# A hybrid decoder layer on one core: chunk after chunk in the first two steps of each group's MLP, post-norm products on GpSimd, and a longer first pause of the decode work

## The chip, the core and the metric

One core of a Trainium2 chip runs the whole layer as one program. The metric is the time of the program on the device, in microseconds (us). Every engine of the core (PE, the matrix engine; DVE, the vector engine; ACT, the scalar engine; POOL, GpSimd; SP, which here only issues transfers) works through its own list of instructions in order, and waits on semaphores for the others.

## The reference

The layer takes 2048 prompt tokens and 32 sample tokens (8 sequences of 4 tokens, each with its own state), 1024 wide, all in fp32. Cut to what matters here, with `x` the tokens and `p` a small input embedding:

```python
xn  = rms_norm(x, norm_mix_pre)
mix = concat(mlstm(xn @ w_in ...), sliding_window_attention(xn @ w_in ...)) @ w_out
x   = x + rms_norm(mix, norm_mix_post)          # a post-norm
u   = rms_norm(x, norm_ffn_pre)
f   = square(relu(u @ w_up)) @ w_down           # 1024 -> 4096 -> 1024
x   = x + rms_norm(f, norm_ffn_post)            # a post-norm
x   = x + sigmoid(x @ w_pgate) * (p @ w_pproj)
```

The sample tokens go through the same layer; their mLSTM and attention read and update given states and caches ("decode").

## The kernel before

**Stages.** The prompt is 16 blocks of 128 tokens. In a first phase, up to about 700 us, all blocks are projected with `w_in`, and mLSTM and attention are computed; their outputs go to DRAM. Then come three groups of two chunks: blocks 0-2 and 3-5 (group 0), 6-8 and 9-11 (group 1), 12-13 and 14-15 with the 32 sample rows (group 2). A group goes through `mix_mm` (the product with `w_out`, matmuls `mo`) and `mix_post` (post-norm, residual, pre-norm and transposes into the tile `ut`) of its first and then its second chunk, then `mlp`, then `gate_post` and `gate_mm` (matmuls `pt`, `pv`, `xt`, `pg`) of both chunks. In group 1 the decode work runs as a side job.

**Precision.** A fp32 number is kept as two fp32r parts, high (`h`) and low (`l`), and each product takes three matmuls (`mm3`, L145): high by high twice over the weights' two parts, and low by high. A helper makes the parts: ACT casts the high one (L228), DVE subtracts (L229); the weights have the same on ACT (L249) and in turns on POOL and DVE (L250).

**Weights.** A ring of 7 buffers holds 512 KB pairs [high|low] of weights. The first time that a weight is used, it is loaded raw on SP's queue, split, and its pair is stored to DRAM by POOL's queue (`wk<-w`, L275). Every later use loads the pair back on SP's queue (`w<-wk`, L282). A plan of all uses in order lets the loads run ahead as buffers come free.

**The MLP.** 16 steps `s` of 256 hidden columns each. For a chunk `ci`, `up(s, ci)` makes 48 matmuls into two tiles of 128 hidden columns; `hidden` takes each through relu and square on ACT (L1617, L1618) and the split (`hh` on ACT, `hl` on DVE); `down(s, ci, half)` makes the `dn` matmuls for one half of the output columns (`dn...t` for the second chunk of group 2, which is computed transposed and carries the sample rows). From step 2 on, `up_both` computes both chunks at once from seven products instead of eight. These need sums and differences of the two chunks' `ut`, which `sums` and `last_sum` make on DVE, ACT and, in groups 1 and 2, for one half of the columns on POOL (L1641 to L1675). The room for them is opened once the decode job is done.

**Steps 0 and 1** are plain. Before, they run in this order: up of step 0 for chunk 0 and its downs, up of step 0 for chunk 1 and its downs; then the sums are started; then up of step 1 for chunk 0, up of step 1 for chunk 1, `last_sum`, and the downs of both. In the sample group the hidden values of 16 of the sample rows are computed with chunk 0 and copied by POOL into chunk 1's tiles (L1624).

**Post-norm.** `finished(b, half, ...)` is called as soon as one half of block b's row is complete: ACT squares it with a running sum (L1441), and it is multiplied in place by the norm's weights (L1443), half 0 on POOL and half 1 on DVE. `rstd` adds on DVE (L1454) and takes the power -0.5 on POOL (L1455). `residual` scales the two halves and adds the block's input, on DVE (L1449).

**What sets the order.** PE's order is written out as the program is built: a model clock `pe.t` advances with each matmul, and side jobs (`swa`, `mls`, `tsp`, `dec`) are generators that yield a number of model microseconds; after each product `tick` runs the next piece of any side job whose time has come, and `drain` runs a job to its end. `tsp` holds post-norms and transposes, `dec` the decode job, which starts with one `yield DECW` and then runs `decode_mlstm` (its first matmuls are `dph`, transposes of the rows `hrow` that a POOL transfer at L1129 brings) and `decode_swa` (`daS`, `daT`, `daO`). The order on the other engines is decided by a scheduler when the program is built.

## Time and profile before

| what | value |
|---|---|
| median of 3 runs | 2674.26 us (2670.22 to 2679.49) |
| the profiled execution | 2676.5 us, of which the span is 2674.7 us |
| mean granted clock of TensorE | 0.981 |
| busy: PE / DVE / ACT / POOL | 95% / 55% / 36% / 25% of the span |
| first matmul of step 0 to first of step 2: group 0 / 1 / 2 | 75.37 / 92.93 / 73.23 us |

A row of the profile's timeline gives the start, the duration, the engine, the line, the operation with output and inputs, how many instructions are taken together, and in brackets how long the engine stood idle before it and what released it. PE is the engine that is nearly always busy, so its idle stretches, and the slow matmuls that follow some of them, are what can be won without computing less.

### The profile page before, as it was taken

The page shows a single profiled execution, that of the slowest core. Times are in us where ns is not written, and L with a number is a line of the kernel's source. Part 1 is how long each engine was busy: PE and PEld are TensorE (multiplying, and loading weights), DVE is VectorE, ACT ScalarE, POOL GpSimd, SP SyncE. Part 2 cuts the span into 40 slices and gives each one's busy share as a digit, 9 for nine tenths or more (in the row PEclk, how much of TensorE's full clock was granted, in tenths as well). Part 3 has the DMA queues.
Part 4 walks back from the last instruction along what each step waited for, and adds up shares of the span by engine and source line. Part 5 has one row for each costly group of instructions (what it writes and reads, how often), then busy time and mean ns, then how long its engine had stood idle before and what let it go on. Part 6 is the DMA issues. An engine that isn't in the chain of part 4 may idle for free.

```text
span 2674.7 us, 39114 instructions
## 1 busy us (share of the span) xinstructions
PE 2549.5 (95%) x14260; PEld 2212.9 (83%) x14260; DVE 1481.7 (55%) x3112; ACT 975.9 (36%) x2165; POOL 658.0 (25%) x936
## 2 busy tenths in 40 slices
PE   7899999998899999999998999999999998999998
PEld 6787878877688888888776789988888877999986
DVE  6675666664677655655735564444446345444443
ACT  5545344543455433444513432222223133222231
POOL 5311111111436666666513320000001012000010
PEclk9999999999999999999998999999999998999999
DMA  8765656666786666666987645555557885777786
GB/s 305 268 215 173 217 167 221 210 241 224 255 326 240 254 245 236 236 236 233 341 323 238 209 142 188 189 189 174 173 182 256 288 316 187 254 261 258 257 297 230
DMA packets 215186, 632.23 MB, mean 236 GB/s; under 512 B 24790, under 2 KB 58794, under 8 KB 214977
## 3 DMA queue, kind: packets, MB, share of 16 engines
q1 hardware_dynamic: 169552, 472.19, 52.0%
q0 software_dynamic: 45392, 157.50, 15.1%
q8 instruction: 113, 1.85, 0.3%
q14 instruction: 81, 0.66, 0.1%
q10 hardware_dynamic: 48, 0.03, 0.0%
HBM read 475.47 MB, written 155.25 MB: 236 GB/s over the span
## 4 chain that ended last, share of the span: by engine, by line
PE 74%; DVE 10%; DMA 6%; issue 4%; POOL 3%; ACT 2%; SPq 0%; POOLq 0%; DVEq 0%; ACTq 0%
PE dn L145 20%; PE up L145 20%; PE pg L145 5%; PE mo L145 5%; PE v L145 3%; DMA wk<-w 3%; PE qk L145 2%; DVE hl L229 2%; DMA w<-wk 2%; PE o L145 2%; PE gv L145 2%; PE qa L145 1%; PE aT L149 1%; PE aO L145 1%; PE pv L145 1%
## 5 line engine op out<-in xcount | busy, mean ns | idle before, releaser
L145 PE MATMUL dn<-w,hh 128*128 128x512 f32 x1792 | 566.6, 397 | 13.7 <-DVE f L1449 5.1
L145 PEld LDWEIGHTS dn<-w,hh 128*128 128x128 f32 x1792 | 333.2, 189 | 95.1 <-DVE f L1728 8.6
L1728 DVE TENSOR_TENSOR f<-f,dn 128x512 f32<-128x512 f32 x420 | 286.9, 687 | 222.0 <-PE dn L145 220.9
L145 PE MATMUL dn<-w,hl 128*128 128x512 f32 x896 | 355.5, 397 | 2.5 <-DVE hl L229 2.4
L1692 DVE TENSOR_TENSOR re<-up,re 128x384 f32<-128x384 f32 (+1 forms) x294 | 152.0, 517 | 326.4 <-PE up L145 326.4
L145 PEld LDWEIGHTS dn<-w,hl 128*128 128x128 f32 x896 | 169.0, 189 | 46.3 <-DVE hl L229 7.5
L1693 ACT COPY re<-up 128x384 f32<-128x384 f32 (+1 forms) x42 | 18.9, 450 | 414.8 <-PE up L145 414.8
L1617 ACT ACTIVATE re<-re 128x384 f32<-128x384 f32 (+1 forms) x168 | 83.2, 495 | 207.9 <-DVE re L1692 205.8
L229 DVE TENSOR_TENSOR hl<-re,hh 128x384 fp32r<-128x384 f32 (+1 forms) x192 | 137.7, 717 | 31.1 <-ACT hh L228 30.4
L275 POOL DMA_DIRECT2D wk<-w x242 | 134.0, 555 | 32.2 <-DVE w L250 29.2
L1443 POOL TENSOR_TENSOR f<-f,gffn 128x512 f32<-128x512 f32 x16 | 21.8, 1365 | 476.5 <-ACT j L1441 476.2
L250 POOL TENSOR_TENSOR w<-wr,w 128x512 fp32r<-128x512 f32 (+2 forms) x76 | 104.9, 1380 | 87.5 <-ACT w L249 86.6
L249 ACT CAST w<-wb 128x512 fp32r<-128x512 f32 x98 | 60.7, 621 | 173.2 <-PE dn L145 118.3
L249 ACT CAST w<-wr 128x512 fp32r<-128x512 f32 (+2 forms) x152 | 89.3, 598 | 85.6 <-PE up L145 34.3
L250 POOL TENSOR_TENSOR w<-wb,w 128x512 fp32r<-128x512 f32 x70 | 91.9, 1313 | 116.3 <-ACT w L249 115.8
L1618 ACT ACTIVATE re<-re 128x384 f32<-128x384 f32 (+1 forms) x192 | 95.1, 495 | 5.9
L228 ACT CAST hh<-re 128x384 fp32r<-128x384 f32 (+1 forms) x192 | 92.8, 483 | 6.8
L1043 ACT ACTIVATE s<-s,swt 128x257 f32<-128x257 f32 (+1 forms) x128 | 63.4, 497 | 77.5 <-DVE swt L1040 76.4
L1037 DVE CUSTOM_DVE_ANT_0 s<-aS,cst,sink 128x256 f32<-128x256 f32 (+1 forms) x128 | 57.0, 473 | 59.4 <-PE aS L145 59.2
L1624 POOL CAST hh<-hh 128x16 fp32r<-128x16 f32 x32 | 8.0, 249 | 319.0 <-ACT hh L228 319.0
L145 PE MATMUL up<-t0h,w 128*128 128x384 f32 (+1 forms) x336 | 85.1, 320 | 0.0
L145 PE MATMUL up<-t1h,w 128*128 128x384 f32 (+1 forms) x336 | 85.1, 320 | 0.0
(1537 smaller groups left out, 6530.7 us busy)
## 6 DMA issues: line engine op xcount, KB each, us to landing
w<-wk SPq DMA_DIRECT2D x692, 512.0 KB, 4.7
wk<-w POOLq DMA_DIRECT2D x238, 512.0 KB, 6.6
wr<-in_w_down_dram SPq DMA_DIRECT2D x64, 256.0 KB, 7.7
wb<-in_w_up_dram SPq DMA_DIRECT2D x28, 512.0 KB, 6.8
w<-wk SPq DMA_DIRECT2D x20, 528.0 KB, 4.4
x<-in_x_prompt_dram SPq DMA_DIRECT2D x16, 512.0 KB, 5.2
y<-yd SPq DMA_DIRECT2D x32, 256.0 KB, 7.1
xr<-in_x_prompt_dram SPq DMA_DIRECT2D x16, 512.0 KB, 6.3
```

What stands on the lines that cost most here:

```text
L145: ins = self.pe.matmul(out, lhsT, rhs, start=start, stop=stop)
L228: act.copy(hi, src)
L229: dve.tensor_tensor(lo, src, hi.bitcast(F32), ALU.subtract)
L249: act.copy(hi, src)
L250: (eng or weng()).tensor_tensor(lo, src, hi.bitcast(F32), ALU.subtract)
L275: here(put(self.kept[key], t.bitcast(U32)))
L1037: dve.tensor_tensor_reduce(s_[:, s, lo : 2 * P], pS[:, s, lo:], bias[:, j, lo:], 1.0 if s == 0 else 0.0625, sink[:, h : h + 1], ALU.add, A ...
L1043: act.activation(e_, e_, AF.Exp, bias=nm[:, s : s + 1], accum_out=sm[:, s : s + 1])
L1617: act.activation(t, src, AF.Relu)
L1618: act.square(t, t)
L1692: add = lambda out, a, b: dve.tensor_tensor(out, a, b, ALU.add)
L1728: dve.tensor_tensor(out(i), out(i), ps[i], ALU.add)
```

## The change

Three things are changed.

- **MLP order.** Steps 0 and 1 are done for chunk 0 first: up and downs of step 0, up and downs of step 1. Then the side jobs are drained, the room for the sums is opened and `sums` is started, and the same four passes are done for chunk 1. `last_sum` follows. The weights of the two steps are thus taken twice: 32 ring tiles a group in place of 20. The downs of step 1 now also begin with three blocks' matmuls on the first hidden tile (`ahead`), as those of step 0 did. In the sample group the 16 rows' hidden values are kept in small tiles between the chunks, with twice as many copies on POOL.
- **Post-norm products.** All products of L1443 go to POOL.
- **Decode's first pause**, `DECW`, is 12 model microseconds in place of 5.

```diff
-FAST = 2, 2, 2
+FAST = 2
-DECW = 5.0
+DECW = 12.0
...
-            for s in range(STEPS):
-                if s >= FAST[gi]:
+            for s in (*range(FAST), *range(STEPS)):
+                if s >= FAST:
...
-                for half in (0, 1, 0, 1) if s == 0 else (0, 1):
+                for half in (0, 1):
...
-        eng = (pool, dve)[half]
-        eng.tensor_tensor(v, v, g[:n, half * 512 : half * 512 + 512], ALU.mult)
+        pool.tensor_tensor(v, v, g[:n, half * 512 : half * 512 + 512], ALU.mult)
...
-            if sample and ci == 1:
-
-                for y, z in zip(hid[0, ft], hid[1, ft]):
-                    pool.tensor_copy(z[:, W : W + HS], y[:, W - HS : W].bitcast(F32))
+            if sample:
+
+                for e, y in enumerate(hid[ci, ft]):
+                    if ci == 0:
+                        t = hid["s", ft, e] = small.tile([P, HS], F32, tag="hs", name=f"hs{e}{nm}", bufs=8)
+                        pool.tensor_copy(t, y[:, W - HS : W].bitcast(F32))
+                    else:
+                        pool.tensor_copy(y[:, W : W + HS], hid["s", ft, e])
...
-            ahead = 3 if s == 0 else 1
+            ahead = 3 if s < FAST else 1
...
-        X = None
-        for s in range(STEPS):
-            hid = {}
-            fast = s >= FAST[gi]
-            if not fast:
-                wu = ring.take(4)
-            if s == 0:
-
-                up(s, 0, wu, hid)
-                for half in range(2):
-                    down(s, 0, half, down_weights(), hid)
-                pe.drain(tsp)
-                up(s, 1, wu, hid)
-                for half in range(2):
-                    down(s, 1, half, down_weights(), hid)
-                continue
-            if s == FAST[gi] - 1:
+        X, hids = None, []
+
+        for ci in range(2):
+            if ci == 1:
+                pe.drain(tsp)
                 pe.drain(dec)
                 es_lp.close()
                 es_t = ExitStack()
                 tp = es_t.enter_context(tc.tile_pool(name="tp", bufs=1, side="right", reuse_waits="tile"))
                 ring.wide = es_t.enter_context(tc.tile_pool(name="wide", bufs=WIDE, side="right", reuse_waits="tile"))
                 tsp.add(sums())
-            if fast:
-                up_both(s, X, hid)
-            else:
-                up(s, 0, wu, hid)
-                up(s, 1, wu, hid)
-                if s == FAST[gi] - 1:
-                    pe.drain(tsp)
-                    last_sum()
+            for s in range(FAST):
+                if ci == 0:
+                    hids.append({})
+                up(s, ci, ring.take(4), hids[s])
+                for half in range(2):
+                    down(s, ci, half, down_weights(), hids[s])
+        pe.drain(tsp)
+        last_sum()
+        for s in range(FAST, STEPS):
+            hid = {}
+            up_both(s, X, hid)
```

Line numbers behind the edits shift: L1443 of before is L1442 after, L1449 is L1448, and from `hidden` on they are three higher.

**PE where the decode job starts**, in group 1's `mix_mm` of chunk 0 (`mo`), before. `yt9t` to `yt11t` are transposes that prepare the next chunk's input, `dph` the first matmuls of decode.

```order
L145 MATMUL mo_14221<-w_14258,yt10l_13906 128x512
L149 MATMUL dph<-ident,hrow 128x24
L149 MATMUL dph<-ident,zqk 128x32
L149 MATMUL dph<-ident,hrow 128x24
L149 MATMUL dph<-ident,zqk 128x32
L149 MATMUL dph<-ident,hrow 128x24
L149 MATMUL dph<-ident,zqk 128x32
L149 MATMUL dph<-ident,hrow 128x24
L149 MATMUL dph<-ident,zqk 128x32
L145 MATMUL mo_14221<-w_14260,yt10h_13904 128x512 x2
L145 MATMUL mo_14221<-w_14260,yt10l_13906 128x512
L149 MATMUL yt9t<-ident,y_14234 128x128 x4
```

And after, at the same place:

```order
L149 MATMUL yt11t<-ident,y_14264 128x128 x4
L145 MATMUL mo_14333<-w_14338,yt10h_13929 128x512 x2
L145 MATMUL mo_14333<-w_14338,yt10l_13931 128x512
L145 MATMUL mo_14334<-w_14336,yt10h_13929 128x512 x2
L145 MATMUL mo_14334<-w_14336,yt10l_13931 128x512
L145 MATMUL mo_14334<-w_14338,yt10h_13929 128x512 x2
L145 MATMUL mo_14334<-w_14338,yt10l_13931 128x512
L145 MATMUL mo_14335<-w_14336,yt10h_13929 128x512 x2
L145 MATMUL mo_14335<-w_14336,yt10l_13931 128x512
L145 MATMUL mo_14335<-w_14338,yt10h_13929 128x512 x2
L145 MATMUL mo_14335<-w_14338,yt10l_13931 128x512
L149 MATMUL dph<-ident,hrow 128x24
```

Between the two places stand 27 `mo` matmuls (9 of the first half, 18 of the other) and the 12 transposes, all of which now run ahead of `dph`.

**POOL in group 0's first post-norm** (`gpost`), before: the products of half 0, the powers (`ms<-ms,nhalf`) on which the residuals wait, and the store of the finished block (`x1d`).

```order
L1443 TENSOR_TENSOR f_7746<-f_7746,gpost_7744 128x512
L1443 TENSOR_TENSOR f_7747<-f_7747,gpost_7744 128x512
L1443 TENSOR_TENSOR f_7748<-f_7748,gpost_7744 128x512
L275 DMA wk_7913<-w_7906 128x1024
L250 TENSOR_TENSOR w_8062<-wr_8064,w_8062 128x512
L275 DMA wk_8043<-w_8036 128x1024
L1455 TENSOR_TENSOR ms_7941<-ms_7941,nhalf 128x1
L1578 DMA out_dram<-cvo 3x512
L275 DMA wk_8069<-w_8062 128x1024
L275 DMA wk_8077<-w_8070 128x1024
L1478 DMA x1d_138<-f_7746 128x1024
L1455 TENSOR_TENSOR ms_7946<-ms_7946,nhalf 128x1
```

And after:

```order
L1442 TENSOR_TENSOR f_7746<-f_7746,gpost_7744 128x512
L1442 TENSOR_TENSOR f_7747<-f_7747,gpost_7744 128x512
L1442 TENSOR_TENSOR f_7748<-f_7748,gpost_7744 128x512
L275 DMA wk_7913<-w_7906 128x1024
L250 TENSOR_TENSOR w_8062<-wr_8064,w_8062 128x512
L275 DMA wk_8043<-w_8036 128x1024
L1442 TENSOR_TENSOR f_7746<-f_7746,gpost_7744 128x512
L1454 TENSOR_TENSOR ms_7941<-ms_7941,nhalf 128x1
L1442 TENSOR_TENSOR f_7747<-f_7747,gpost_7744 128x512
L1577 DMA out_dram<-cvo 3x512
L1442 TENSOR_TENSOR f_7748<-f_7748,gpost_7744 128x512
L275 DMA wk_8069<-w_8062 128x1024
```

The product of half 1 of a block now stands ahead of that block's power, and the next block's ahead of the next.

**DVE in group 2's plain MLP steps**, before: `ts`, `t0l`, `t1l` and `t2l` belong to `sums`, `tl` to `last_sum`, and `hl` is the low part of a hidden tile, here that of step 0 for chunk 1.

```order
L1647 TENSOR_TENSOR ts_21025<-ut21h_20679,ts_21024 128x4x136
L1659 TENSOR_TENSOR t0l_21019<-ts_21024,t0h_21018 128x4x136
L1649 TENSOR_TENSOR ts_21025<-ts_21025,ut21l_20681 128x4x136
L1651 TENSOR_TENSOR ts_21026<-ut20h_20419,ts_21025 128x4x136
L1659 TENSOR_TENSOR t1l_21021<-ts_21025,t1h_21020 128x4x136
L1653 TENSOR_TENSOR ts_21026<-ut20l_20421,ts_21026 128x4x136
L1659 TENSOR_TENSOR t0l_21019<-ts_21168,t0h_21018 128x4x136
L229 TENSOR_TENSOR hl_20888<-re_20884,hh_20887 128x272
L1659 TENSOR_TENSOR t2l_21023<-ts_21026,t2h_21022 128x4x136
L1659 TENSOR_TENSOR t1l_21021<-ts_21169,t1h_21020 128x4x136
```

And after, where the `hl` rows are those of step 1 for chunk 0:

```order
L237 TENSOR_TENSOR ut21l_20728<-g_20940,ut21h_20726 128x4x16
L237 TENSOR_TENSOR ut21l_20729<-g_20944,ut21h_20727 128x4x16
L1654 TENSOR_TENSOR ts_21062<-ut20h_20467,ts_21061 128x4x136
L229 TENSOR_TENSOR hl_20952<-re_20948,hh_20951 128x272
L1656 TENSOR_TENSOR ts_21062<-ut20l_20469,ts_21062 128x4x136
L1662 TENSOR_TENSOR t1l_21057<-ts_21061,t1h_21056 128x4x136
L1662 TENSOR_TENSOR t0l_21055<-ts_21060,t0h_21054 128x4x136
L1662 TENSOR_TENSOR t2l_21059<-ts_21062,t2h_21058 128x4x136
L229 TENSOR_TENSOR hl_20988<-re_20984,hh_20987 128x272
```

The chain of the sums that stood ahead of the hidden tiles of step 0 of chunk 1 now stands ahead of those of step 1 of chunk 0.

## Prediction

> **What bounds the kernel now.** I read the page's busy times and the chain of waits first.
>
> ```profile
> span 2674.7 us, 39114 instructions
> PE 2549.5 (95%) x14260; PEld 2212.9 (83%) x14260; DVE 1481.7 (55%) x3112; ACT 975.9 (36%) x2165; POOL 658.0 (25%) x936
> PE 74%; DVE 10%; DMA 6%; issue 4%; POOL 3%; ACT 2%; SPq 0%; POOLq 0%; DVEq 0%; ACTq 0%
> ```
>
> PE is busy for 95% of the span, and the change leaves its matmuls as they are in number and shape. So it can only win or lose where PE stands still or runs slowly. The reader needs PE's undisturbed pace for that; the chain, cut to the MLP steps, gives it (start, duration, what, how many):
>
> ```profile
> 1599.62 14.74 PE up L145 x84
> 1614.36 16.71 PE dn L145 x72
> 2246.97 12.07 PE up L145 x96
> 2259.04 5.57 PE dn L145 x24
> 2264.61 3.20 PE dn210t L145 x24
> ```
>
> An up matmul takes 14.74 / 84 = 0.175 us, a dn 0.232; in group 2 an up takes 0.126 and a transposed dn 0.133. Next, the stretches that the change rewrites, as a table of windows (elapsed, then PE busy; the granted clock stands behind the engines; last DMA share and GB/s): the first two MLP steps of the three groups, the start of decode, and the end of group 2's `mo`.
>
> ```profile
> 775.64:851.01 75.37, 71.33 (x362) 62.59 (x360) 63.37 (x89) 41.72 (x77) 32.64 (x33) 1.00 0.67 236
> 1506.53:1599.46 92.93, 87.87 (x454) 73.30 (x453) 61.18 (x94) 43.63 (x90) 21.12 (x15) 0.98 0.44 149
> 2197.59:2270.82 73.23, 58.28 (x361) 53.68 (x360) 41.44 (x67) 26.00 (x58) 17.80 (x19) 0.86 0.54 183
> 1404.00:1421.00 17.00, 7.97 (x34) 5.95 (x32) 6.52 (x24) 2.31 (x5) 10.75 (x22) 0.60 0.51 149
> 2177.00:2197.60 20.60, 19.23 (x89) 14.85 (x88) 11.28 (x27) 7.66 (x17) 4.02 (x4) 0.92 0.98 382
> ```
>
> Group 0's window holds 192 up and 144 dn, 33.6 + 33.4 us, and some 2.4 us of transposes: 69.4, so about 6.0 are lost. Group 2's holds 192 up, 48 dn, 96 transposed dn and 2.4 us of transposes: 24.2 + 11.1 + 12.8 + 2.4 = 50.5, so 22.7 are lost. Group 1's also holds decode; its loss is counted below.
>
> **The change part by part.**
>
> *Decode's first pause.* PE's timeline, with the idle time ahead of an instruction and its releaser in brackets, and POOL's transfer that is waited for, with its landing time:
>
> ```profile
> 1403.96 0.40 PE L145 MATMUL mo<-w,yt10l 128*128 128x512 f32 x1
> 1413.38 0.27 PE L149 MATMUL dph<-ident,hrow 24*128 24x24 f32 x1 [9.03 <-DMA hrow<-in_state_mlstm_conv_dram]
> 1414.34 1.22 PE L145 MATMUL mo<-w,yt10h 128*128 128x512 f32 x2
> 1420.99 0.71 PE L145 MATMUL mo<-w,yt10h 128*128 128x512 f32 x2
> 1405.50 0.52 POOL L1129 DMA_DIRECT2D hrow<-in_state_mlstm_conv_dram x1
> DMA to landing us min/median/max: 7.8/7.8/7.8
> ```
>
> PE stands still for 9.03 us, because `hrow` is issued at 1405.50 and lands 7.8 us later. From 1413.38 to 1420.99, 7.61 us, it does 9 mo, 12 transposes and ten small matmuls slowly (two mo in 1.22 us; the window's clock is 0.60). At pace that is 9 x 0.232 + 12 x 0.108 + 1.1 = 4.5 us: 3.1 more are lost, 12.1 in all. In the new order 27 mo and the 12 transposes run ahead of `dph`: 27 x 0.232 + 1.3 = 7.6 us. POOL's transfers do not wait for them, so `hrow` lands when it did. The wait shrinks to about 1.5 us, and I allow 0.6 us of slow matmuls behind it. **Gain 10.0** (8.5 if a short wait leaves the clock low for longer, 10.6 if it leaves it alone).
>
> By the Trainium skill ("TensorE: Matmul & The Clock Gate", Part 1, the HAM clock gate) PE falls to half clock after an idle window of about 3.4 us, and needs about as long of busy time to come back; that would make the slow part worth 1.7 us, an estimate, and the gain 7.5 + 1.7 = 9.2. The trace agrees that the clock falls, but the slow matmuls last 7.6 us here and cost 3.1, and the trace's number is used.
>
> Two later waits of decode may move with it:
>
> ```profile
> 1458.19 3.58 PE L145 MATMUL dpX<-scs,sqm 128*32 128x130 f32 x16 [2.34 <-issue]
> 1477.97 0.71 PE L145 MATMUL dpU<-sva,skm 32*128 32x130 f32 x4 [2.40 <-DVE skm L1275]
> ```
>
> The first stands behind four residuals on DVE, which the new order places ahead of decode's own DVE work. **Gain 1**, from -2 (the waits come in pairs) to 4.7 (both go).
>
> *Chunk order in the MLP, group 2.* PE's waits there, and SP's transfer behind the first:
>
> ```profile
> 2208.85 1.19 PE L145 MATMUL dn<-w,hh 128*128 128x512 f32 x2 [5.08 <-DVE f L1449]
> 2221.96 0.39 PE L145 MATMUL up<-ut21h,w 128*128 128x272 f32 x1 [2.34 <-ACT ut21h L236]
> 2223.72 0.60 PE L145 MATMUL up<-ut21l,w 128*128 128x272 f32 x1 [1.37 <-DVE ut21l L237]
> 2235.11 0.40 PE L145 MATMUL dn200t<-hh,w 128*128 128x288 f32 x1 [1.18 <-ACT re L1617]
> 2239.83 0.58 PE L145 MATMUL dn200t<-hh,w 128*128 128x288 f32 x1 [4.06 <-issue]
> 2200.55 0.90 SPq L1429 DMA_DIRECT2D xr<-in_x_prompt_dram x2
> ```
>
> First wait, 5.08: the second hidden tile's `hl` on DVE stands behind residuals that wait for `xr`, which SP issues right behind `gffn`, whose place is freed by the last post-norm product. It stays, and that product ends 0.7 us later on POOL (rows below): 5.8. Second, `ut21`: 2.34 + 1.37, and the 48 up behind it take from 2223.72 to 2232.37, 8.65 us where 6.0 would do: 6.4 in all. With chunk 1's up a whole step later, about 12 us of PE work, this goes. Third, dn200t: 1.18 + 4.06 + 0.4, and slow matmuls, about 8: the hidden tiles' `hl` stand behind the sums. The sums now stand ahead of step 1's hidden tiles of chunk 0 in DVE's list, so this wait moves and is paid there, about 8 again. New are two downs that follow their own up without cover: the hidden tile takes ACT relu, square, cast and DVE's subtraction, four times about 0.5 us, and 9 matmuls on the first tile cover 1.2 us of it, so about 1.1 each. Sum: -6.4 + 0.7 + 2.2 = -3.5. **Gain 3.5** (from -2, if the sums cost twice, to 9, if they fit beside the matmuls).
>
> *Group 1.* PE's waits and one of the sums' steps on POOL:
>
> ```profile
> 1578.38 0.73 PE L145 MATMUL dn<-w,hh 128*128 128x512 f32 x2 [2.31 <-ACT hh L228]
> 1583.77 0.73 PE L145 MATMUL dn<-w,hh 128*128 128x512 f32 x2 [2.29 <-ACT re L1617]
> 1574.06 2.43 POOL L1653 TENSOR_TENSOR ts<-ut10l,ts 128x768 f32<-128x768 f32 x1
> ```
>
> The 72 dn of step 1 run from 1575.22 to 1599.46, 24.2 us for 16.7: 7.5 are lost to the sums, seven steps of 2.4 us in a row on POOL. The sums now start before chunk 1's first up and have 33 us of chunk 1's matmuls beside them, in place of 17. But they stand between this chunk's hidden tiles on ACT and DVE (about 2.5 lost at its first down), `last_sum` must wait for the last up of chunk 1 and goes ahead of the last hidden tile (about 3), and the end of decode, drained in front of chunk 1, has no matmuls between its transposes and `daO` (about 2). Sum 7.5. **0** (-5 to 4).
>
> *Group 0.*
>
> ```profile
> 788.27 0.73 PE L145 MATMUL dn<-w,hh 128*128 128x512 f32 x2 [1.03 <-ACT hh L228]
> 797.99 0.45 PE L145 MATMUL up<-ut01l,w 128*128 128x384 f32 x1 [0.85 <-DVE ut01l L237]
> 811.30 0.50 PE L145 MATMUL dn<-w,hl 128*128 128x512 f32 x1 [1.89 <-DVE hl L229]
> ```
>
> The wait at 797.99 goes; the first down waits longer, because two more POOL products stand ahead of the second chunk's first power (2.6, less what DVE is spared, about 2.3); the new downs lose about 0.5 each. **Loss 1** (-4 to 3).
>
> *Products on POOL.* From the list of groups, one product:
>
> ```profile
> L1443 POOL TENSOR_TENSOR f<-f,gpost x16: 1286/1298/1730, 722.7 to 2185.1; 128x512 f32<-128x512 f32 x16
> L1443 DVE TENSOR_TENSOR f<-f,gpost x16: 669/682/694, 738.3 to 2199.4; 128x512 f32<-128x512 f32 x16
> ```
>
> 1.30 us on POOL for 0.68 on DVE. Where a block's residual waits for its own second product this adds 0.6 to 1.3 us; it takes 0.68 us off DVE. The starts of the MLPs have it already. At the groups' gates PE waits on DVE:
>
> ```profile
> 1306.21 0.66 PE L149 MATMUL xt10t<-ident,f 128*128 128x128 f32 x4 [2.90 <-DVE xt00l L229]
> 2618.43 0.80 PE L149 MATMUL xt150t<-ident,f 128*128 128x128 f32 x4 [4.14 <-DVE xt21l L229]
> ```
>
> Behind both, DVE runs products and residuals one after the other, while POOL has gaps. Freed of two or three products, 1.4 to 2.0 us, against 0.6 to 1.3 us of later products, DVE is ready about 0.5 us sooner. **Gain 1.5** over three groups (-4 to 4).
>
> *Reloads.* Twelve more per group, 36 of 512 KB:
>
> ```profile
> w<-wk SPq DMA_DIRECT2D x692, 512.0 KB, 4.7
> ```
>
> They cost nothing while the ring's seven buffers are filled in time. In group 2's passes of chunk 1, 8 tiles are used in 48 x 0.126 + 48 x 0.133 = 12.4 us: 8 x 0.524 MB / 12.4 us = 338 GB/s. The window ahead of that group moved 382 GB/s. In groups 0 and 1 it is 8 tiles in 16.8 us, 250 GB/s. So the matmuls hide them, narrowly in group 2; without that cover the price is the rival below.
>
> Sum: 10 + 1 + 3.5 + 0 - 1 + 1.5 = **15 us gained**. The profiled execution took 2676.5 us, 2.2 more than the median; the same saving from the median gives 2674.3 - 15 = **2659 us**.
>
> **The rivals.**
>
> *The gain stays in decode and the MLP gives it back.* For it: the two plain steps have six more places where a down follows its own up, and each can cost what the row at 811.30 shows (1.89) or the one at 2235.11 (1.18), not the half of it. Six times 1.5 is 9, 5 more than the 4 or so that I count; the sums costing twice in group 2 take 5.5 more. The gain is 15 - 10.5 = 4.5: 2670 us, no change. Against it: the first hidden tile's matmuls now cover part in every down.
>
> *POOL becomes the pace of every post-norm: slower.* One mechanism: POOL takes a chunk's products in order, so with six products at 1.30 ahead of the powers, each residual comes up to 3.9 us later. It decides once a chunk's last power ends after DVE would have been free. At nine places (the six chunks' gates and the three MLP starts) a delay of 2.6, two products, and 1 us of slow matmuls costs 32; with the gains at decode and group 2's ut21 (10 + 6.4) left, 2674 + 16 = 2690. For it: POOL in group 1 also issues decode's stores, between the products. Against it: POOL is 25% busy, and the order places a block's products and power together.
>
> The Trainium skill ("GPSIMD Engine Reference", 4.1, Engine selection) puts elementwise work on VectorE and calls GpSimd about twice as slow for two inputs, which is the direction of this rival. The two rows of L1443 agree, 1.30 against 0.68 us.
>
> *The reloads set the pace.* If the transfers of groups 1 and 2 ran no faster than their windows show (149 and 183 GB/s), 32 tiles of 0.524 MB would take 113 and 92 us, 20 and 22 more than I forecast for the windows, and the time would be 2659 + 42 = 2701 us, slower. Against it: those rates are demand, and 382 was reached 20 us earlier.
>
> *The change moves less than it says.* If `hrow` were itself issued later by what `dph` is moved, the wait would stay and the whole gain be 5: 2669 us, no change. Against it: POOL's list has the same instructions ahead of `hrow`.
>
> **How the numbers follow.** A difference under about 0.3%, 8 us, cannot be told from none with this kernel's spread: 2666 to 2682 is "the same". My forecast has 0.62, and its own range, by the ends of the terms that are least certain (3 to 5 each way, not all together), is 2648 to 2667. The MLP that gives back has 0.16, the unmoved `hrow` 0.05, POOL's pace 0.12, the reloads 0.05. Faster: 0.64, the forecast and a little of the second case; same: 0.22; slower: 0.14. The range reaches to the no-change cases: 2648 to 2678.
>
> **What would show it.** The bracket ahead of the first `dph` under 3 us, with a clock of 0.9 or more in the 17 us around it. No wait for `ut21` in group 2, and its window near 70 us; windows near 76 and 93 us in groups 0 and 1. The waits ahead of `xt10t` and `xt150t` no longer than now. Wrong would be the forecast if brackets with POOL L1442 or L1454 appear in front of transposes or ups, if `DMA w<-wk` releases PE in chunk 1's passes, or if the `dn` behind the ups of step 1 wait more than 3 us each.

## The result, and the profile after

The changed kernel takes 2695.8 us (median of four runs, 2694.3 to 2697.9), the kernel before 2674.5 (2670.2 to 2679.5): a ratio of 1.008 with the interval 1.006 to 1.010. It is slower by 21 us, where I had forecast a gain of 15; the time lies outside the range. A few single executions, of this program and of others below, took much longer (up to 8103 us); medians and ratios leave them out.

The first lines of the page of the changed kernel:

```profile
span 2692.5 us, 39307 instructions
PE 2557.6 (95%) x14260; PEld 2215.3 (82%) x14260; DVE 1465.8 (54%) x3078; ACT 974.2 (36%) x2165; POOL 710.1 (26%) x1034
```

The span is 17.8 us longer than before. 8 us of this are more busy time of PE for the same 14260 matmuls, so slower matmuls; the rest is more standing still. DVE has lost 34 instructions and 15.9 us, POOL has gained 98 and 52.1.

To find the place, both spans were cut at the same matmuls (first `mo` of group 0's second chunk, first `mo` of group 1, first `up` of an MLP, first matmul on the sum tile `t1` in step 2, and so on; this last one stands 24 matmuls into step 2, so the windows of the plain steps are 3 to 4 us longer than the prediction's). These are the windows of the kernel before in which something changed (columns as in the prediction: elapsed, PE, PEld, DVE, ACT, POOL, granted clock, DMA share, GB/s):

```profile
739.10:775.64 36.54, 36.47 (x171) 29.45 (x169) 21.15 (x41) 17.20 (x35) 14.80 (x19) 1.00 0.91 345
775.64:855.20 79.56, 75.52 (x385) 66.78 (x384) 64.06 (x90) 43.47 (x80) 36.79 (x38) 1.00 0.65 230
1397.93:1603.65 205.72, 186.89 (x922) 149.68 (x921) 116.37 (x239) 76.80 (x164) 64.21 (x84) 0.94 0.61 199
2197.59:2273.84 76.25, 61.30 (x385) 56.70 (x384) 41.89 (x68) 26.39 (x59) 17.80 (x19) 0.87 0.55 189
2273.84:2668.04 394.20, 387.90 (x2516) 355.30 (x2514) 187.00 (x381) 101.07 (x233) 21.53 (x70) 1.00 0.74 262
```

And the same windows of the changed kernel, with a sixth that lies inside the third:

```profile
736.34:780.76 44.42, 39.28 (x171) 31.65 (x169) 20.38 (x39) 17.56 (x35) 18.55 (x23) 0.92 0.79 284
780.76:869.96 89.20, 80.34 (x385) 69.93 (x384) 63.38 (x86) 43.02 (x80) 33.71 (x41) 0.94 0.78 276
1414.36:1622.44 208.08, 193.57 (x923) 153.57 (x922) 112.45 (x233) 76.47 (x164) 71.85 (x90) 0.93 0.70 227
2218.13:2288.74 70.61, 58.52 (x386) 52.65 (x385) 38.36 (x66) 26.18 (x59) 20.32 (x29) 0.95 0.84 298
2288.74:2686.08 397.34, 388.36 (x2516) 355.74 (x2514) 187.64 (x376) 100.92 (x233) 42.88 (x131) 0.99 0.74 260
1497.00:1513.00 16.00, 15.89 (x40) 11.36 (x41) 3.26 (x11) 0.59 (x1) 3.69 (x5) 0.50 0.38 103
```

From the top: the `mo` of group 0's second chunk is 7.9 us longer; group 0's two plain MLP steps 9.6 longer; group 1 from its first `mo` to step 2, with all of decode, 2.4 longer; group 2's plain steps 5.6 shorter; the passes at the end, with the last gate in them, 3.1 longer. The sixth row is a surprise. For 16 us in the middle of decode PE is busy all the time at a granted clock of 0.50.

PE's timeline of the changed kernel shows what it waits for in these places:

```profile
756.89 1.22 PE L145 MATMUL mo<-w,yt01h 128*128 128x512 f32 x2 [5.07 <-DMA w<-wk]
...
1429.75 0.24 PE L149 MATMUL dph<-ident,hrow 24*128 24x24 f32 x1 [1.42 <-DMA hrow<-in_state_mlstm_conv_dram]
...
1497.11 1.23 PE L145 MATMUL dpU<-sva,skm 32*128 32x130 f32 x4 [3.00 <-DVE skm L1275]
...
2636.41 1.11 PE L149 MATMUL xt150t<-ident,f 128*128 128x128 f32 x4 [5.42 <-DVE xt21l L229]
```

The wait for `hrow` is 1.42 us, where it was 9.03. Against it stand a wait for a weight reload in group 0 that was not there before (5.07), the wait for `skm` with the slow stretch behind it (3.00, before 2.40), and a longer wait at the last gate (5.42, before 4.14).

### The profile page after: what moved, and what is told of

The parts are those of the page before. It is cut to its first block, busy times and chain, and to the rows that moved or that the text cites. A ratio compares the mean times of both kernels' runs of the same rounds, so it can differ in the third digit from the quotient of the medians.

```text
span 2692.5 us, 39307 instructions
## 1 busy us (share of the span) xinstructions
PE 2557.6 (95%) x14260; PEld 2215.3 (82%) x14260; DVE 1465.8 (54%) x3078; ACT 974.2 (36%) x2165; POOL 710.1 (26%) x1034
## 4 chain that ended last, share of the span: by engine, by line
PE 41%; issue 3%; DVE 3%; DMA 2%; POOL 1%; ACT 1%; SPq 0%; POOLq 0%; DVEq 0%; ACTq 0%
PE up L145 15%; PE dn L145 12%; PE pg L145 4%; PE mo L145 3%; PE pv L145 1%; DMA w<-wk 1%; POOL f L1442 0%; DVE f L1448 0%; DMA hrow<-in_state_mlstm_conv_dram 0%; DMA out_dram<-ot 0%; PE dpU L145 0%; POOL ms L1454 0%; POOL out_dram L1804 0%; DMA xr<-in_x_prompt_dram 0%; ACT j L1441 0%
## 5 line engine op out<-in xcount | busy, mean ns | idle before, releaser
L1442 POOL TENSOR_TENSOR f<-f,gffn 128x512 f32<-128x512 f32 x32 | 41.2, 1296 | 472.8 <-ACT j L1441 472.3
L1696 ACT COPY re<-up 128x384 f32<-128x384 f32 (+1 forms) x42 | 18.9, 450 | 403.0 <-PE up L145 403.0
L1625 POOL COPY hs<-hh 128x16 f32<-128x16 f32 x32 | 11.1, 346 | 301.9 <-ACT hh L228 301.9
L145 PE MATMUL up<-t2h,w 128*128 128x384 f32 (+1 forms) x336 | 85.1, 320 | 0.0
```

The lines of the kernel that those rows point to most:

```text
L145: ins = self.pe.matmul(out, lhsT, rhs, start=start, stop=stop)
```

## The experiments

All medians below stand beside the kernel before on the same chip (2673 to 2676 us), and ratios have their 95% interval. The table gives each stage's difference to the kernel before, in us, from one profiled execution of each kernel; the columns are explained with the runs.

| stage | before | whole change | E1 | E2 | E3 | E4 | E5 | E8 |
|---|---|---|---|---|---|---|---|---|
| group 0, `mo` of the second chunk | 36.5 | +7.9 | -0.6 | +8.1 | -0.1 | +0.2 | -0.1 | +0.1 |
| group 0, plain MLP steps | 79.6 | +9.6 | -0.1 | +2.1 | +10.2 | +10.2 | 0.0 | -0.1 |
| group 0's gate, up to group 1's `mo` | 104.6 | +1.7 | -0.4 | -0.8 | -1.0 | -1.2 | +0.3 | 0.0 |
| group 1, `mo` of both chunks, decode, plain steps | 205.7 | +2.4 | -0.9 | -6.5 | +3.7 | -4.5 | -6.3 | -2.8 |
| group 1's gate, up to group 2's `mo` | 103.9 | +2.8 | -0.7 | +4.4 | +0.3 | -0.5 | -0.4 | -0.5 |
| group 2, plain MLP steps | 76.3 | -5.6 | +0.3 | +1.6 | -5.4 | -5.9 | -6.0 | +0.9 |
| group 2's fast passes and gate | 394.2 | +3.1 | +0.1 | +3.6 | +0.2 | +0.3 | 0.0 | -1.7 |

Stages that are left out change by up to 3 us from one execution to the next, whatever the kernel, so a column doesn't add up to the difference of the medians.

### One part at a time: E1 to E4

**E1, decode's first pause alone**, in the kernel before:

```diff
-DECW = 5.0
+DECW = 12.0
```

> The kernel before with decode's first pause at 12 and nothing else. In the trace of the whole change the wait ahead of dph shrank from 9.03 to 1.42 us and that stretch gained 9.6 us, but the rest of decode in group 1's mix stage lost 10.6 (waits of 2.05 for a weight reload, 1.64 for DVE, 3.00 for skm with a long stretch at half clock behind it). Theory A, the products on POOL are what delayed the rest: here about 10 us are gained, 2664 us. Rival B, a later start of decode only moves its waits along: 2670 to 2676 us, with new waits at dpc, dpX or dpU of the size that was saved.

Measured: 2674.1 us against 2674.0, ratio 0.9999 (0.9988 to 1.0010). The pause does what was predicted and is worth nothing by itself. PE's timeline of E1:

```profile
1410.13 0.24 PE L149 MATMUL dph<-ident,hrow 24*128 24x24 f32 x1 [0.58 <-DMA hrow<-in_state_mlstm_conv_dram]
...
1575.08 1.22 PE L145 MATMUL dn<-w,hh 128*128 128x512 f32 x2 [7.34 <-ACT re L1617]
```

The 9.03 us at `dph` are down to 0.58. But the two waits at the end of decode, where the sums begin, were 2.31 and 2.29 and are now 7.34 and 3.08. With them and some smaller waits in decode, the stage is 0.9 us shorter in place of 10. PE gains 12.8 us up to the second chunk's `mo`, but decode itself does not end sooner: POOL's first step of the sums, which wait for decode's end, starts 156.8 us after group 1's first `mo` in E1 and 157.9 before. So the matmuls that now fill the first pause are missing later, and the sums have less beside them.

**E2, all products of the post-norms on GpSimd, alone**:

```diff
-        eng = (pool, dve)[half]
-        eng.tensor_tensor(v, v, g[...], ALU.mult)
+        pool.tensor_tensor(v, v, g[...], ALU.mult)
```

> The kernel before with all post-norm products on POOL and nothing else. In the order built for it, SP's list has the xr load of group 0's second post-norm six reloads earlier, as in the whole change, where PE then waited 5.07 us for a reload. Theory A, this edit is the larger part of the loss: group 0's second half of mix costs 8 us more, its first downs 4 to 6 more, the gates 3 to 6 more, in sum 15 to 20, 2690 to 2694 us. Rival B, the chunk order in the MLP carries the loss: within 5 us of before, 2670 to 2680 us.

Measured: 2692.8 us, ratio 1.0072 (1.0054 to 1.0089): 18.9 us slower. This one edit costs nearly as much as the whole change. By the table it brings group 0's wait for a reload (+8.1 in that stage, as in the whole change) and the longer gates of group 1 (+4.4) and group 2 (+3.6). E2's gain of 6.5 us in group 1 was not explained; the wait at `dpX` (2.34) is gone there, and that at `dph` is 1.1 us shorter.

**E3, the new order of chunks alone** (`FAST`, the two loops, the copies of the sample rows, `ahead`; `DECW` 5, products as before).

> Only the new chunk order of the two plain MLP steps with its reloads, pause 5, products as before. From the windows of the whole change: group 2's two steps gain 5.6, group 1's lose 1.4, group 0's lose about 4 (the wait at the last down) if their other 6 us come from the POOL products. Theory A: about 2674 us, no change. Rival B, the order itself carries group 0's whole 9.6 and part of the later gates: 2680 to 2686 us.

Measured: 2677.8 us, ratio 1.0014 (1.0003 to 1.0024). Group 2 gains 5.4, group 1 loses 3.7, and group 0 loses 10.2, where I had predicted a loss of 1 for it.

**E4, the change without the products**: the changed kernel with the line `eng = (pool, dve)[half]` put back.

> The whole change with half 1 of the products back on DVE. Theory A, POOL's products cost 15 to 20 us: 2677 to 2681 us if decode's gain is lost in any case, 2664 to 2670 us if POOL also ate that gain. Rival B: 2690 us or more. SP's list has xr where it was before, so no wait for a reload is expected in group 0's mix.

Measured: 2673.9 us, ratio 0.9999 (0.9986 to 1.0012). Without the products the change is worth nothing, and with them it costs 21 us. In group 1 the two parts need each other: the pause alone gives -0.9, the order alone +3.7, both together -4.5. Group 0 keeps its loss of 10.2, so this loss isn't caused by the post-norm's products.

### Why products on GpSimd cost so much: E6, E7, E8, E11, E12

The theory after E2: a product on POOL costs more than its own 1.30 us, since DVE can't do its elementwise work beside it. The rival: the product is merely late, and the residual behind it waits. The kernel before already shows the first in its fast MLP passes; DVE's timeline, and then POOL's, in the same 6 us:

```profile
928.29 2.62 DVE L229 TENSOR_TENSOR hl<-re,hh 128x384 fp32r<-128x384 f32 x1
...
932.37 1.47 DVE L229 TENSOR_TENSOR hl<-re,hh 128x384 fp32r<-128x384 f32 x1
...
934.35 0.55 DVE L229 TENSOR_TENSOR hl<-re,hh 128x384 fp32r<-128x384 f32 x1
```

```profile
927.92 1.31 POOL L307 TENSOR_TENSOR wb<-wb 128x512 f32<-128x512 f32 x1
929.18 1.30 POOL L306 TENSOR_TENSOR wb<-wb,wb 128x512 f32<-128x512 f32 x1
932.12 1.30 POOL L313 TENSOR_TENSOR wb<-wb,wb 128x512 f32<-128x512 f32 x1 [1.64 <-DVE w L250]
```

The subtraction `hl` takes 0.55 us with POOL quiet (934.35). The one at 932.37 starts 0.25 us into a POOL operation and ends at 933.84, which is 0.42 after POOL's end (932.12 + 1.30 = 933.42). The one at 928.29 meets two in a row, and ends 0.43 after the second (930.48). So the DVE operation doesn't run slowly, it stands still until POOL has no more of them. Over the whole trace of the kernel before, `hl` has a median of 1.47 us under a POOL product, and the ops of L1659 (128x768) take up to 2.61 in place of 0.95. Operations with one input in PSUM (L1728, L1692, L1534) take 0.69, 0.56 and 0.75 us with POOL busy or quiet.

The Trainium skill ("SBUF — State Buffer", Who interferes with whom) says just this: a VectorE instruction with two inputs in SBUF contends with a GpSimd instruction that reads SBUF, the later one blocks fully until the other is done, and one with at most one SBUF input, outside its two-port modes, is left alone. The rows agree, 0.55 against 1.47 us and 0.69 against 0.69.

**E11, an extra product**: the kernel before, all of whose work is left in, with one more POOL product for each second half, which multiplies the gains by themselves into the unused half of ACT's scrap tile `j`, which nothing reads.

```diff
         eng.tensor_tensor(v, v, g[...], ALU.mult)
+        if half == 1:
+            w = g[:n, half * 512 : half * 512 + 512]
+            pool.tensor_tensor(junk[:n, 512:], w, w, ALU.mult)
```

> Before, with one more product on POOL for each half 1: norm weights by norm weights into a scrap tile that nothing reads. The real product of half 1 stays on DVE, so no residual waits for a later product. Beside the stage windows of e2_pool this tells what of the loss is POOL's time and its contention with DVE, and what is the later product. Contention theory: the gates of groups 1 and 2 lose most of what they lost in e2 (4.4 and 5 us): 2682 us or more. Rival, the chain through the product: the gates lose less than 2 us each, 2674 to 2678 us.

Measured: 2684.5 us, ratio 1.0042 (1.0029 to 1.0055). The real products stay where they were, and the chain from a product to its residual has not become longer by an operation of its own; still it costs about 10 us. The busy times of E11's page, and then its PE timeline at the last gate:

```profile
PE 2552.0 (95%) x14260; PEld 2214.3 (83%) x14260; DVE 1492.8 (56%) x3112; ACT 974.9 (36%) x2165; POOL 690.3 (26%) x970
```

```profile
2622.73 1.11 PE L149 MATMUL xt150t<-ident,f 128*128 128x128 f32 x4 [5.65 <-DVE xt21l L229]
```

DVE has the same 3112 instructions as before and is busy for 11.1 us more (1481.7 before), and the last gate's wait is 5.65 (4.14), as in the whole change. By stages, group 0's `mo` is unchanged (-0.1), its plain steps lose 2.6, the gates of groups 0 and 1 2.5 and 1.9, the last stage 3.2. So the moved product's own place in the chain is not needed for the loss. The run is not quite pure: at the first two gates ACT's next square waits for the scrap tile (2.85 and 2.24 us). The last gate has no such wait, and its powers are not held up: POOL stands idle for 2.02 us ahead of one until DVE has added. There the blocked DVE alone is enough.

**E8, all products on DVE**, in the kernel before (`dve.tensor_tensor` in both halves).

> Before, with all products on DVE, none on POOL. In the trace of before a residual or hi-lo subtraction with both inputs in SBUF takes 0.55 us, and 1.47 us while POOL multiplies or subtracts. Theory, POOL's products cost DVE more time than they take from it: 2 to 8 us faster, 2666 to 2672 us, above all at the gates. Rival, one product more on DVE, 0.68 us, costs what it takes: 2676 to 2682 us.

Measured: 2669.1 us, ratio 0.9976 (0.9964 to 0.9988): a small gain, from the opposite of the edit. The busy times of E2's page and then of E8's, and E8's PE timeline at the last gate:

```profile
PE 2550.2 (95%) x14260; PEld 2213.5 (82%) x14260; DVE 1473.2 (55%) x3078; ACT 974.8 (36%) x2165; POOL 698.3 (26%) x970
PE 2545.5 (95%) x14260; PEld 2211.7 (83%) x14260; DVE 1486.2 (56%) x3146; ACT 974.7 (37%) x2165; POOL 612.3 (23%) x902
```

```profile
2609.60 1.11 PE L149 MATMUL xt150t<-ident,f 128*128 128x128 f32 x4 [2.62 <-DVE xt21l L229]
```

In E8 DVE does 34 more instructions than before; 32 of them, products at 0.68 us, are 21.8 us, but it is busy for only 4.5 us more. The other 17 us were time in which it had stood blocked. In E2 it does 34 fewer, some 23 us, and is busy for only 8.5 less (1481.7 before), so some 14 came back. The gate's wait falls from 4.14 to 2.62. The groups of the residual, in the changed kernel and then in E8, show both costs (busy, mean ns of one, idle before it and what ended it):

```profile
L1448 DVE SCALAR_TENSOR_TENSOR f<-f,ms,x 128x512 f32<-128x512 f32 x32 | 28.3, 904 | 0.2
L1448 DVE SCALAR_TENSOR_TENSOR f<-f,ms,xr 128x512 f32<-128x512 f32 x32 | 26.6, 879 | 11.9 <-DMA xr<-in_x_prompt_dram 6.0 <-POOL ms L1454 5.9
```

```profile
L1448 DVE SCALAR_TENSOR_TENSOR f<-f,ms,x 128x512 f32<-128x512 f32 x32 | 23.4, 761 | 0.1
L1448 DVE SCALAR_TENSOR_TENSOR f<-f,ms,xr 128x512 f32<-128x512 f32 x32 | 23.3, 777 | 4.3 <-DMA xr<-in_x_prompt_dram 4.3
```

The residual is blocked in the changed kernel (904 and 879 ns against 761 and 777), and it waits 5.9 us for POOL's powers, which are queued behind the products; in E8 it doesn't wait for them at all. The rows that scale a power (`ms<-ms,rq`) wait for it too. DVE's waits for powers, in the changed kernel and then before (total us, times, longest):

```profile
DVE ms L1793 <- POOL ms L1454: 11.1, 14, 2.2
DVE f L1448 <- POOL ms L1454: 5.9, 5, 2.0
```

```profile
DVE ms L1799 <- POOL ms L1455: 2.3, 5, 0.7
```

That makes 17.0 us against 2.3, and 4.4 in E11. So the later powers are a second cost, of like size in DVE's time, and the runs do not part the two in E2.

**E6 and E12, second halves on POOL only for the gates' products** (with the weights `gffn`), in the kernel before:

```diff
-        eng = (pool, dve)[half]
+        eng = dve if half and g is gpost else pool
```

> Before, with half 1 of the products on POOL only for the MLP's post-norm (gffn); those of the mix stage (gpost) as before. xr is back in its old place in SP's list. Theory: group 0's mix (8 us) and first steps (2) do not lose; the gates lose what they lost with all products on POOL, about 4.4 in group 1, 5 in group 2 from step 2 to the end, and under 2 in group 0: 2682 to 2686 us. Rival, the gates' loss came from the disturbed start: 2674 to 2677 us.

> Again the kernel of e6_gffnpool, for a profile that can be read: group 0's mix as before (36.5 us from its second half to the first up), the gates of groups 1 and 2 later by about 4 and 5 us as with all products on POOL.

Measured: E6 2687.8 us, ratio 1.0038 (1.0023 to 1.0053). E12 is the same kernel, one execution of 2683.6 us, and gives the stages. Half of the products give about half of the loss. In E12 the `mo` of group 0's second chunk is as before (36.7), while group 1's gate is longer by 3.4 and the last stage by 3.6. So the `gffn` products make the gates' loss, and the products of the other post-norm make group 0's 8 us.

**E7, a fourth load buffer**, in E2's kernel. The 8 us in group 0 are a reload that is late, and SP's waits in the changed kernel (725 to 790 us) say why; the columns are total us, times, longest:

```profile
SPq L282 <- DMA wk<-w: 9.2, 2, 8.8
SPq L1429 <- DVE ms L1453: 8.5, 1, 8.5
```

SP issues its transfers in order. In the new order of its list the load of `xr` stands six reloads earlier than before, and it waits 8.5 us for the place that a DVE operation frees; the reload that PE needs stands behind it. With one buffer more that place should be free in time: that was the theory. The rival: the reload waits for the store of its own weight.

```diff
-LBUF = 3
+LBUF = 4
```

> All products on POOL and nothing else, with a fourth buffer for xr, so that xr's load on SP's queue need not wait for the residual that frees its buffer. Theory, SP stood at xr for 8.5 us and the weight reloads behind it came late: the 5.07 us wait of PE in group 0's mix goes and that stage returns to within 1 us of before; 2684 to 2687 us. Rival, the reload was late because POOL stored its weights late: the wait stays, 2692 us.

Measured: 2693.7 us, ratio 1.0067 (1.0052 to 1.0082), no better than E2, and what the rival expected. Still, PE's wait was halved, to 2.78 us. The wait that SP keeps there (SP's waits, 725 to 795 us):

```profile
SPq L282 <- DMA wk<-w: 8.4, 2, 6.3
```

The stage came down from 44.6 us in E2 to 40.6 (36.5 before). The wait for `xr` is gone, and SP still stands 6.3 us for a store. The timelines of POOL and SP in the changed kernel show that this store is also what PE's reload waits for last there:

```profile
740.87 1.31 POOL L1442 TENSOR_TENSOR f<-f,gpost 128x512 f32<-128x512 f32 x1
742.11 1.15 POOL L275 DMA_DIRECT2D wk<-w  x2
```

```profile
750.69 0.32 SPq L282 DMA_DIRECT2D w<-wk  x1
```

SP sends `xr` at 740.62 and two reloads behind it, and then stands 8.8 us, until a store has landed. POOL issues this store behind its third product of a second half, and it lands 8.6 us later; the reload is issued at once and lands at 756.85, and PE goes on at 756.89. In the kernel before, the store is issued 2.7 us after the stage's first `mo` (5.8 in the change) and lands after 3.0. So the product in POOL's list holds the store up by some 3 us, and its slow landing costs more; why it lands so slowly was not found. Of the 4 us that E7 wins in this stage, group 0's gate (+0.3 for E2's -0.8) and group 1 (-4.5 for -6.5) take 3 back; why is open.

### Why group 0 loses 10 us by the order: E10, E14

Theory: step 1's weights are used for the first time now beside chunk 1's post-norm, and each needs a raw load, a cast on ACT and a subtraction, on DVE or POOL in turn; where POOL does it, DVE's `hl` and `ut01l` are blocked. The rival: the downs simply follow their own up too closely. DVE's timeline of E4, then POOL's, then PE's:

```profile
787.51 2.05 DVE L237 TENSOR_TENSOR ut01l<-g,ut01h 128x512 fp32r<-128x512 f32 x1
789.49 2.27 DVE L229 TENSOR_TENSOR hl<-re,hh 128x384 fp32r<-128x384 f32 x1
```

```profile
787.72 1.28 POOL L250 TENSOR_TENSOR w<-wr,w 128x512 fp32r<-128x512 f32 x1
...
790.06 1.27 POOL L250 TENSOR_TENSOR w<-wr,w 128x512 fp32r<-128x512 f32 x1
```

```profile
791.82 0.80 PE L145 MATMUL dn<-w,hl 128*128 128x512 f32 x1 [3.49 <-DVE hl L229]
```

`hl` ends at 791.76, again 0.43 us after POOL's end, and PE goes on at once.

**E10**: E3, with these subtractions all on DVE in group 0's plain steps.

```diff
+        if wfix[0] is not None:
+            return wfix[0]
...
+        wfix[0] = dve if gi == 0 else None
```

> As e3_mlp (only the new chunk order), but during the two plain steps of group 0 all subtractions that make the weights' low parts run on DVE, none on POOL. In e4_nopool the hl subtraction in front of PE's longest wait there, 3.49 us, took 2.27 us beside such a subtraction on POOL, and takes 0.55 us alone. Theory, contention with POOL: that subtraction goes back to 0.55 us, the waits at the first down fall from 4.9 to about 2 us, and group 0's two steps from 89.7 to about 86 us. Rival, the mere number of first-use casts and subtractions ahead of the hidden tiles: with eight more of them on DVE the two steps take 90 us or more.

Measured: 2668.3 us, ratio 0.9976 (0.9967 to 0.9985), 9.4 us under E3. The stage falls from 89.7 to 81.8, and in DVE's timeline of E10 the same operation takes its plain time:

```profile
785.01 0.55 DVE L229 TENSOR_TENSOR hl<-re,hh 128x384 fp32r<-128x384 f32 x1
```

So some 8 of the 10.2 us go with POOL's subtractions. In this stage DVE is busy for 62.2 us with 95 instructions, against 65.4 with 90 in E3, so blocked time went; that the subtraction itself is also quicker on DVE (0.69 us against 1.28) is not parted from it. The rival keeps at most the last 2.

**E14**: the same edit in a kernel with group 0 in the old order (E9 below), to see whether there was anything to win there.

> The version of e9_combo, and in group 0's two plain steps (old order) all subtractions for the weights' low parts on DVE, as e10_mlpdve had them in the new order. There the stage went from 89.7 to 81.8 us. Contention theory: group 0's two steps still hold three waits of 0.9 to 1.9 us at hl and ut01l in the old order; they shrink by 2 to 4 us in sum, 2655 to 2657 us. Rival, in the old order nothing on POOL runs beside them: 2659 us as e9_combo.

Measured: 2658.4 us, ratio 0.9942 (0.9927 to 0.9957); E9 has 0.9944 (0.9931 to 0.9957), so no difference, and the 2 to 4 us of the theory did not come: the stage takes 78.6 us against 79.5 in E9. In the old order PE hardly waits for what these subtractions block; in the new order it does.

### What is left of the change that pays: E5, E9

**E5**: group 0 in the old order, groups 1 and 2 in the new one, `DECW` 12, products as before the change.

```diff
-            for s in (*range(FAST), *range(STEPS)):
+            for s in (*range(FAST), *range(STEPS)) if gi else range(STEPS):
...
-        pool.tensor_tensor(v, v, g[...], ALU.mult)
+        eng = (pool, dve)[half]
+        eng.tensor_tensor(v, v, g[...], ALU.mult)
```

> Group 0 in the old order of its two plain steps, groups 1 and 2 in the new one, pause 12, products on POOL and DVE in turn as before. By the windows of the parts: in the run of the whole change without POOL's products group 0's two steps lost 10.2 us, group 1 from its first mo to step 2 gained 4.5, group 2's two steps 5.9. Theory: the parts add by stage, and group 0 goes back to its old time: a gain of 10 us, 2664 us. Rival, group 1's gain came from what group 0 left behind in the queues: 2669 to 2674 us.

Measured: 2665.0 us against 2676.2, ratio 0.996 (0.9947 to 0.9973). PE at the end of decode in E5, where E1 had waited 7.34 and 3.08 (two more waits follow, of 1.16 and 2.34):

```profile
1567.17 0.50 PE L145 MATMUL dn<-w,hl 128*128 128x512 f32 x1 [1.72 <-DVE hl L229]
```

The sums now have both steps of chunk 1 beside them. This is the 6.3 us in group 1 and the 6.0 in group 2 of the table.

**E9**: E5 with all products on DVE.

> The version of e5_hybrid (group 0's old order, groups 1 and 2 new, pause 12) with all products on DVE as in e8_alldve. The gains measured alone are 0.40% and 0.24%. Theory, they lie in different stages and add: 2658 to 2661 us. Rival, group 1's gain in e5 and e8 is the same one: 2664 to 2666 us.

Measured: 2658.8 us against 2674.9, ratio 0.9944 (0.9931 to 0.9957). E9 and E14 are faster than the kernel before by some 15 us.

### The slow stretch again: E13

**E13** is the whole change, unaltered, in a second profiled execution.

> The whole change once more, for a second profile. In the first, PE ran at a granted clock of 0.50 from 1497 to 1513 us behind a wait of 3.00 us, about 8 us lost, while the same wait in e1_decw and e4_nopool was followed by some 3 us of slow matmuls. If the stretch belongs to the kernel it is there again; if it belongs to one execution, the clock is back within 6 us of the wait and group 1 is about 5 us shorter.

Measured: 2695.1 us. A window of its profile:

```profile
1495.50:1512.50 17.00, 16.97 (x43) 12.16 (x44) 3.21 (x10) 0.59 (x1) 3.61 (x5) 0.50 0.39 106
```

The stretch at half clock comes back at the same place, so it belongs to this kernel's timing, as far as two executions show. At half pace 16 us are 8 lost; without them group 1's stage would be 200.1 us, like E4's 201.2. In E4 the same wait for `skm`, 3.00 us too, ends at 1487.12; the window of 16 us behind it:

```profile
1487.12:1503.12 16.00, 16.00 (x65) 11.92 (x66) 3.48 (x11) 1.76 (x3) 6.28 (x11) 0.89 0.54 170
```

65 matmuls are done there and only 40 in the slow stretch. What makes the difference stays open.

## Why the prediction was wrong, point by point

**Products on POOL** is the step that failed first. It said that DVE, "freed of two or three products", would be ready about 0.5 us sooner at each gate: gain 1.5. Measured alone (E2): a loss of 18.9. I had counted a product at 1.30 us on POOL and 0.68 on DVE, as if the two engines worked independently. The traces show that DVE's operations with two SBUF inputs stop while POOL has one; so more than half of what was taken off DVE came back as blocked time (E2: some 14 of 23 us; E8, the other way, 17 of 21.8). That could have been read from the kernel before, where `hl` takes 0.55 us in one place and 2.62 in another; I used means. Two more costs stand beside it. The powers are queued behind the products, and DVE waits 17.0 us for them in place of 2.3; the prediction had this delay in its account of group 0 and in a rival, and not in this term. And in group 0's `mo` a weight's store stands behind the products in POOL's list and `xr` ahead of six reloads in SP's: the reload comes late, which is 8.1 us of E2's loss and was at nothing in the sum. How the gates' loss divides between blocked DVE and later powers stays open.

**Group 0**, "Loss 1", measured 10.2 (E3, E4). I counted the waits that go and come at the downs, and missed that the first use of step 1's weights moves beside chunk 1's post-norm. E10 takes back about 8 by moving only those weights' subtractions from POOL to DVE.

**Decode's first pause.** The wait was predicted well, 1.5 against 1.42. Behind it PE ran at a granted clock of 0.50 for some 3.4 us (1431.8 to 1435.1), about 1.7 lost where I had allowed 0.6. The gain of 10 did not come: alone it gives 0.9 in its stage (E1), because I ended the account at `dph` and did not ask what the matmuls that were pulled forward had covered before. **Group 1**, "0", is +3.7 alone and cannot be added to decode's term: both together give 4.5 (E4), for the 11 that the sum had with **dpX and dpU**. At dpU the wait of 2.40 did not go but became 3.00; the one at dpX went, and new ones came ahead of `mo` (2.05, for a reload) and `dpd` (1.64).

**Group 2** had the mechanism right and the size low: 3.5 predicted, 5.4 to 5.9 measured in E3, E4 and the change. No wait there is ended by `ut21` any more, as foreseen. What moved with the sums, and the new downs, cost less than the 10 us that I had counted for them: the waits there come to 5.6 us in the changed kernel (0.90, 1.22, 0.52, 1.39 and 1.55).

**Reloads** were rightly put at nothing: group 2's window moved 298 GB/s (189 before), and no wait for a reload stands in chunk 1's passes. Two waits for a reload came elsewhere. That of 5.07 us in group 0's `mo` comes with the products (E2 has it, with 5.59) and that of 2.05 in group 1's `mo` with the pause (E1 has it, with 2.06), and in neither run are there more reloads.

By the steps: 20.4 us were missed on the products, 9.2 in group 0, 6.5 in decode and group 1 together; 2.1 came better in group 2. That makes 34.0 of the 36.3 between the forecast gain of 15 and the loss of 21.3. That the sum comes so near is in part luck, since the parts are not additive by stage: in group 1, E2 (-6.5) and E4 (-4.5) together would give -11.0, and the change has +2.4. The half-clock stretch is 8 us of this.

Of the rivals, **POOL becomes the pace of every post-norm** came nearest: 2690 against 2695.8, with a chance of only 0.12. It had the queue of products ahead of the powers as its mechanism, which is there; the blocking of DVE and the late store it did not have, and it counted gains at decode that did not come. That the MLP gives the gain back was true in group 0, for a reason that rival did not name. Of the signs that I had listed, the bracket at `dph` and group 2's window came as forecast (67.6 us, cut as in the prediction). Group 0's window (85.0 for about 76) and the wait of `xt150t` showed where it failed. None of those that name POOL or a reload in chunk 1's passes appeared: POOL's cost reached PE through DVE.

## What to carry to other kernels

Before elementwise work goes from DVE to POOL, look in the trace for one DVE form with two SBUF inputs at its shortest and its longest, and at what POOL does beside the long ones: that difference, not POOL's low share, is the price. When matmuls are pulled forward into a pause, name the later wait that they used to cover, and test two such edits both alone and together. And look at the in-order list of every engine that issues transfers: here a store behind POOL's products, and a load that waits for its buffer on SP, stood ahead of the reload that PE needed.

## What the runs showed of the hardware that I had not expected

A DVE operation with two SBUF inputs waits out not one POOL operation but a whole row of them (2.62 us for 0.55, with two POOL products of 1.3 back to back), and ends 0.42 to 0.43 us after the last. In E4 `hl` did so although its row starts 0.57 us ahead of POOL's row.

PE ran at a granted clock of 0.50 for 16 us while it was busy for 99% of them, after a wait of 3.00 us, in both profiles of the change. The Trainium skill ("TensorE: Matmul & The Clock Gate", Part 1, the HAM clock gate) has the clock come back after about 3.4 us of sustained work; here 16 us were not enough. In E4 a clock of 0.89 over the 16 us behind the same wait is 1.8 us lost, what some 3.5 us at half pace cost, as the page has it.
